# Sending the second head pair of four RWKV products to the other half of the array's columns

## The chip, the cores and the metric

The kernel runs on one core of one Trainium2 chip. Its time is the device time of that core in microseconds (us). Three runs of the kernel before took 2783.94, 2780.48 and 2779.83 us; the median is 2780.48 us. TensorE (called PE in the profile) multiplies matrices on an array of 128 x 128 cells and writes to PSUM, a memory of eight banks of 2 KB in each of 128 partitions. ScalarE (ACT) and VectorE (DVE) read PSUM and write SBUF, the main on-chip memory. A matmul may use a part of the array: the rows are given by the partitions from which its operands are read, the columns by the PSUM partitions to which its result goes.

## The reference, cut to what matters

One decoder layer over 2048 tokens of width 1024: a norm, one input projection, two groups of heads side by side (HGRN2, 4 heads of 128, and RWKV-7, 8 heads of 64), an output projection, and a feed-forward part with a short convolution. Everything is float32. The change touches RWKV-7 alone, whose recurrence is

```python
def step(S, inp):
    rt, wt, kt, vt, at, bt = inp
    sa = jnp.einsum('bhvk,bhk->bhv', S, at)
    S = S * wt[:, :, None, :] + sa[..., None] * bt[:, :, None, :] + vt[..., None] * kt[:, :, None, :]
    y = jnp.einsum('bhvk,bhk->bhv', S, rt)
    return S, y
```

## The kernel before

The kernel has two phases. Phase 1 (about the first 1400 us) makes the input projection, the two kinds of heads and the output projection; phase 2 is the feed-forward part, which the change doesn't touch.

Phase 1 is written as three Python generators. `dense` issues the projections: for each block of 512 tokens and each group of 128 output columns, 24 matmuls of 128x512 (L259 to L261: each float32 product is made of three products of rounded parts, which ACT and DVE split at L243 and L244 into `wh` and `wl`). `rw_stream` runs RWKV, `hg_stream` runs HGRN2. A loop takes one step (up to the next `yield`) of the RWKV generator, one of the HGRN2 generator, and then lets `dense` issue work worth `TICK` = 2000 ns. The framework's scheduler then orders the instructions of each engine once more, at build time, so instructions can move across the steps; at run time each engine works its list in order, and waits where an operand or a buffer isn't ready.

PSUM is split by tags: two banks for `dense` (`pj`), two for HGRN2 (`hg`), and two buffers of two banks each for RWKV (`rw`, taken by `bank2()`). A third `bank2()` waits until the reader of the first is done.

RWKV goes in eight steps called `rw_super`, two for each block of 512 tokens. One takes four heads, as two head pairs `u` = 0, 1 (a pair fills 128 partitions, head `h` = 0, 1 in it), and eight chunks of 64 tokens, numbered by `b` = 0 to 3 and `e` = 0, 1. Within a chunk the recurrence becomes a triangular system of 64 x 64, which is inverted. Matrices of chunk `e` live on the partitions 64 to 127 for `e` = 0 and 0 to 63 for `e` = 1 (`er0(e)` gives the first one). Each `rw_super` has four products that the change touches, each with one small matmul for every `(u, b, h, e)`, 32 in all:

- `lv` (L742): 64 rows by 64 columns of the array, 64 elements streamed. The rows begin at `kr`, the columns at `er0(e)`; one ACT instruction of 128x1024 copies the result to `RHS`.
- `z` (L786) and `z2` (L800): 32 rows by 32 columns, 32 streamed, which join the two inverted 32 x 32 halves of the triangular matrix. After each, two ACT instructions (one for each `e`) of 32x512 copy the result, to `TZ` and to `TTs`.
- `qu` (L814): 64 rows by 64 columns, 128 streamed. Head pair 0 is done first into one `bank2()`, and copied by three ACT instructions (one to `M`, two to `UV`), then a `yield`, and head pair 1 likewise, with a `yield` of its own.

In all four, both head pairs use the same two parts of the array: for `lv` and `qu` two of the four 64 x 64 quadrants, one for each `e`. The order within each product is all matmuls of head pair 0, then all of head pair 1.

After `qu` comes `yg` (L834): for each `u`, 32 matmuls of 64 rows by 64 columns with 64 streamed (16 with `M` as the streamed operand, 16 with `KBT`). In it the rows go by `e` and the columns by `h`, so that all four quadrants are used. `yg` of head pair 0 takes the `bank2()` that `qu` of head pair 0 held, and `yg` of pair 1 that of pair 1. Then come `xp` and `yp` (L850, L857), and the carry from chunk to chunk (L868, L870).

Between `lv` and `z` lies the inversion of the 32 x 32 blocks on DVE (31 pairs of instructions), and transfers through DRAM.

Of the kernel before, what the change touches and what calls it, by code (L numbers as in the profile page):

```python
# [11 lines left out]
AF = mybir.ActivationFunctionType  # L12
# [6 lines left out]
P = 128  # L19
# [42 lines left out]
def tile_layer(ctx, tc, consts, x, norm1_w, w_in, hg_lb_logits, hg_norm_w, rw_shift_mu, rw_w0, rw_w2,  # L62
# [4 lines left out]
    V, S, TE = nc.vector, nc.scalar, nc.tensor  # L67
# [41 lines left out]
    def act(out_, in_, func, **kw):  # L109

        want = tables.get(func)
        if want is not None and want != tab["now"]:
            pre = S.preload_act_table_set(want)
            for u_ in tab["uses"]:
                tc.add_manual_dep(pre.ins, u_.ins.name, NOSYNC, reason="table order")
            tab.update(now=want, pre=pre, uses=[])
        i_ = S.activation(out_, in_, func, **kw)
        if want is not None:
            tc.add_manual_dep(i_.ins, tab["pre"].ins.name, NOSYNC, reason="table order")
            tab["uses"].append(i_)  # L120
        return i_
# [141 lines left out]
    def phase1(c1):  # L263
# [14 lines left out]
        TTs = hp.tile([P, 16, 64], F32, name="TTs")  # L278
# [324 lines left out]


        er0 = lambda e: 64 if e == 0 else 0
        c16 = lambda t_: t_.rearrange("p u (c t) -> p (u c) t", t=64)
        v16 = lambda t_: t_.rearrange("p u (b e t) -> p (u b) e t", e=2, t=64)
        U = range(2)

        def rw_super(nb, s_):  # L610
# [6 lines left out]
            def tile_(tag, shape, name):  # L617
                return rp.tile([P] + shape, F32, tag=tag, name=name)

            def bank2():  # L620
                return ps.tile([P, 2, BLK], F32, tag="rw", name="rw", bufs=2)
# [3 lines left out]
            bs_ = [bank2() for _ in U]  # L625
            for u in U:
                TE.matmul(bs_[u][:, 0, :], w2a2[64:128, pc[u]], tl[64:128, :], start=True, stop=True)
            for u in U:
                TE.matmul(bs_[u][:, 1, :], w2a2[0:64, pc[u]], tl[0:64, :], start=True, stop=True)
            for u in U:  # L630
                act(a[:, u], bs_[u][:, 0, :], AF.Sigmoid, bias=vec("a0", prs[u]))
# [47 lines left out]
            M = tile_("M", [2, 2, 4, 2, P], "M")  # L679
            for j in range(2):  # L680
                for u in U:
                    s1 = bank2()
                    for i in range(4):
                        b, e = 2 * j + i // 2, i % 2
# [13 lines left out]
            for u in U:  # L698
                for e in range(2):
                    for q in range(2):  # L700
                        r0 = er0(e) + 32 * q
# [13 lines left out]
            RHS = tile_("KB", [8, 2, P], "RHS")  # L715
            UV = tile_("UV", [8, 2, P], "UV")
# [15 lines left out]
            yield  # L732

            lv = bank2()
            for u in U:
                for b in range(4):
                    for h in range(2):
                        for e in range(2):
                            kr = 0 if e == 0 else 64
                            r0 = er0(e)  # L740
                            sl = (b * 2 + h) * 64
                            TE.matmul(lv[r0:r0 + 64, u, sl:sl + 64], M[kr:kr + 64, u, e, b, h, 0:64],  # L742
                                      UV[kr:kr + 64, 4 * u + b, e, h * 64:h * 64 + 64], start=True, stop=True,
                                      tile_position=(kr, r0))
            act(RHS[:, :, :, 64:128], lv.rearrange("p u (b h t) -> p (u b) h t", h=2, t=64), AF.Copy)
            yield

            n = 64
# [17 lines left out]
            TZ = tile_("XH", [2, 2, 4, 2, 32], "TZ")  # L766
            for u in U:
                for e in range(2):
                    r0 = er0(e)
# [7 lines left out]
            for _ in range(2):  # L777
                yield
            z = bank2()
            for u in U:  # L780
                for b in range(4):
                    for h in range(2):
                        for e in range(2):
                            r0 = er0(e)
                            sl = u * 256 + (b * 2 + h) * 32
                            TE.matmul(z[r0 + 32:r0 + 64, 0, sl:sl + 32], M[r0:r0 + 32, u, e, b, h, 32:64],  # L786
                                      TZ[r0:r0 + 32, 0, u, b, h, :], start=True, stop=True,
                                      tile_position=(r0, r0 + 32))
            for e in range(2):
                r1 = er0(e) + 32  # L790
                act(TZ[r1:r1 + 32, 1].rearrange("p u b h t -> p (u b h t)"), z[r1:r1 + 32, 0, :], AF.Copy)
            yield
            z2 = bank2()
            for u in U:
                for b in range(4):
                    for h in range(2):
                        for e in range(2):
                            r0 = er0(e)
                            sl = u * 256 + (b * 2 + h) * 32
                            TE.matmul(z2[r0:r0 + 32, 0, sl:sl + 32], TZ[r0 + 32:r0 + 64, 1, u, b, h, :],  # L800
                                      TTs[r0 + 32:r0 + 64, u * 8 + b * 2 + h, 32:64], start=True, stop=True,
                                      tile_position=(r0 + 32, r0))
            for e in range(2):
                r0 = er0(e)
                act(TTs[r0:r0 + 32, :, 32:64], z2[r0:r0 + 32, 0, :].rearrange("p (s t) -> p s t", t=32), AF.Copy)
            yield
            for u in U:
                qu = bank2()
                for b in range(4):
                    for h in range(2):  # L810
                        for e in range(2):
                            r0 = er0(e)
                            sl = ((b % 2) * 2 + h) * P
                            TE.matmul(qu[r0:r0 + 64, b // 2, sl:sl + P], TTs[r0:r0 + 64, u * 8 + b * 2 + h, :],  # L814
                                      RHS[r0:r0 + 64, 4 * u + b, h, :], start=True, stop=True,
                                      tile_position=(r0, r0))
                quv = qu.rearrange("p j (b h t) -> p (j b) h t", h=2, t=P)
                bs = slice(4 * u, 4 * u + 4)
                act(M[:, u, 0, :, :, 0:64], quv[:, :, :, 0:64], AF.Copy)
                act(UV[64:128, bs, 0, :].rearrange("p b (h t) -> p b h t", t=64), quv[64:128, :, :, 64:128], AF.Copy)  # L820
                act(UV[0:64, bs, 1, :].rearrange("p b (h t) -> p b h t", t=64), quv[0:64, :, :, 64:128], AF.Copy)
                yield
            for u in U:
                Q, G = M[:, u, 0, :, :, 0:64], M[:, u, 1, :, :, 0:64]
                yg = bank2()
                for w in range(2):
                    for b in range(4):
                        for e in range(2):
                            rs_ = slice(er0(e), er0(e) + 64)
                            sl = w * 256 + b * 64  # L830
                            for h in range(2):
                                rhs = (M[rs_, u, e, b, h, 64:128] if w == 0
                                       else KBT[rs_, u, 2 * b + e, h * 64:h * 64 + 64])
                                TE.matmul(yg[h * 64:h * 64 + 64, e, sl:sl + 64], Q[rs_, b, h, :], rhs,  # L834
                                          start=True, stop=True, tile_position=(er0(e), h * 64))
# [10 lines left out]
            for u in U:  # L846
                for ch in range(8):
                    b, e = ch // 2, ch % 2
                    for h in range(2):
                        TE.matmul(xp[h * 64:h * 64 + 64, u, ch * 64:ch * 64 + 64], KBT[:, u, ch, h * 64:h * 64 + 64],  # L850
                                  UV[:, 4 * u + b, e, h * 64:h * 64 + 64], start=ch == 0, stop=False,
                                  tile_position=(0, h * 64), skip_group_check=True)
            for u in U:
                for ch in range(8):
                    b, e = ch // 2, ch % 2
                    for h in range(2):
                        TE.matmul(yp[h * 64:h * 64 + 64, u, ch * 64:ch * 64 + 64],  # L857
                                  UV[:, 4 * u + b, e, h * 64:h * 64 + 64], M[:, u, e, b, h, 64:128], start=ch == 0,
                                  stop=False, tile_position=(0, h * 64), skip_group_check=True)
            yield  # L860
            WC2 = WC.rearrange("p (u c) t -> p u c t", u=2)
            for ch in range(8):
                b, e = ch // 2, ch % 2
                cs_ = slice(ch * 64, ch * 64 + 64)
                for u in U:
                    for h in range(2):
                        hr = slice(h * 64, h * 64 + 64)
                        TE.matmul(xp[hr, u, cs_], M[hr, u, 1, b, e, 0:64], XH[hr, u, ch, :], start=False,  # L868
                                  stop=ch == 7, tile_position=(h * 64, h * 64), skip_group_check=True)
# [3 lines left out]
            for u in U:  # L873
                for ch in range(8):
                    cs_ = slice(ch * 64, ch * 64 + 64)
                    for h in range(2):
                        hr = slice(h * 64, h * 64 + 64)
                        TE.matmul(yp[hr, u, cs_], XH[hr, u, ch, :], RT[hr, u, ch, :], start=False, stop=ch == 7,
                                  tile_position=(h * 64, h * 64), skip_group_check=True)
# [186 lines left out]
    if "1" in stages:  # L1066
        with ExitStack() as c1:
            phase1(c1)
# [15 lines left out]
    with ExitStack() as c2:  # L1084
# [35 lines left out]
        with tc.tile_pool(name="op", bufs=1, reuse_waits="tile") as op_:  # L1120
# [4 lines left out]
            b = NBLK - 1  # L1125
# [248 lines left out]
    with tc.tile_pool(name="dn", bufs=1, reuse_waits="tile") as dn:  # L1374
# [59 lines left out]
        for s_ in range(3, N):  # L1434
            g, p, kk = steps[s_]
# [53 lines left out]
```

## Time and profile before

| | |
|---|---|
| time of three runs, median | 2780.48 us |
| profiled execution: span from the first to the last instruction (the page gives no other time for it) | 2783.2 us |
| PE busy over the span | 2678.8 us, 96% |
| ACT busy over the span | 1421.1 us, 51% |
| PE busy in phase 1 (0 to 1400 us) | 1335.72 us |
| mean granted TensorE clock | 0.984 of full speed |

A group of the profile is one line of the kernel on one engine with one shape; its row gives the count, the busy time, the mean duration of one in ns, and the idle time just ahead. A matmul that the code writes in float32 is two records in the trace, so 32 matmuls of `lv` are 64 records, and eight `rw_super` have 512. Ends of matmuls are modelled and overlap, so the pace of a burst is read from the start of its first to the start of what follows. A row of the timeline gives start, duration, engine, line, operation, shape and count, and in brackets how long the engine had been idle and for whom.

### The profile page before, as it was taken

How to read it: one execution, taken by the hardware profiler on the slowest of the kernel's cores; microseconds unless marked ns; L12 is line 12 of the kernel's file. 1: busy time of each engine (PE TensorE's matmuls, PEld its weight loads, DVE VectorE, ACT ScalarE, POOL GpSimd, SP SyncE). 2: the span in 40 equal slices, each digit the busy share in tenths (PEclk: the TensorE clock that was granted, in tenths of full speed). 3: DMA queues.
4: the chain of work that ended last, by engine and by line, in shares of the span. 5: the costliest groups of instructions: out<-in, count | busy, mean ns of one | idle time of the engine just before them, and what ended most of it. 6: DMA issues, size and time to landing. Idle time of an engine off the chain costs nothing.

```text
span 2783.2 us, 47784 instructions
## 1 busy us (share of the span) xinstructions
PE 2678.8 (96%) x18059; PEld 2135.2 (77%) x18059; DVE 2066.4 (74%) x3877; ACT 1421.1 (51%) x2254; POOL 11.1 (0%) x24
## 2 busy tenths in 40 slices
PE   8999999989999999999989999998999999999998
PEld 6877777767787777777767888886888888877887
DVE  4867778685686766868658789989997877677656
ACT  5445454544646446435346765456455555445444
POOL 0000000000000000000000000000000000000000
PEclk9999999999999999999899999999999999999999
DMA  5222322244441344543475457756672223998855
GB/s 163 72 69 72 99 73 78 63 131 141 131 121 58 102 141 136 161 132 94 131 239 178 143 172 262 239 165 216 205 245 88 87 76 135 324 333 310 289 193 186
DMA packets 429628, 435.01 MB, mean 156 GB/s; under 512 B 68703, under 2 KB 288213, under 8 KB 429397
## 3 DMA queue, kind: packets, MB, share of 16 engines
q1 hardware_dynamic: 428337, 429.30, 48.4%
q8 instruction: 142, 2.33, 0.3%
q0 software_dynamic: 992, 2.64, 0.2%
q14 instruction: 89, 0.73, 0.1%
q10 hardware_dynamic: 68, 0.02, 0.0%
HBM read 325.94 MB, written 105.91 MB: 155 GB/s over the span
## 4 chain that ended last, share of the span: by engine, by line
PE 78%; DVE 7%; ACT 7%; DMA 4%; issue 3%; SPq 1%; DVEq 0%; ACTq 0%
PE pj L259 8%; PE pj L260 8%; PE pj L261 8%; PE ua L261 6%; PE ua L259 5%; PE ua L260 5%; PE ud L259 3%; PE ud L260 3%; PE ud L261 3%; PE da L260 2%; PE da L261 2%; PE da L259 2%; PE hg L948 2%; PE db L259 2%; PE db L260 2%
## 5 line engine op out<-in xcount | busy, mean ns | idle before, releaser
L259 PE MATMUL pj<-hh,wh 128*128 128x512 f32 x960 | 401.8, 419 | 0.9 <-DVE xh L398 0.4
L260 PE MATMUL pj<-hl,wh 128*128 128x512 f32 x960 | 379.9, 396 | 0.0
L261 PE MATMUL pj<-hh,wl 128*128 128x512 f32 x960 | 379.0, 395 | 0.2 <-DVE wl L244 0.2
L243 ACT CAST wh<-wraw 128x512 fp32r<-128x512 f32 x240 | 147.0, 619 | 307.9 <-PE pj L260 266.2
L259 PE MATMUL ua<-Bh,uwh 128*128 128x512 f32 x704 | 278.6, 396 | 15.0 <-ACT uwh L243 13.7
L261 PE MATMUL ua<-Bh,uwl 128*128 128x512 f32 x704 | 276.6, 393 | 0.7 <-DVE uwl L244 0.7
L260 PE MATMUL ua<-Bl,uwh 128*128 128x512 f32 x704 | 276.5, 393 | 0.0
L244 DVE TENSOR_TENSOR wl<-wraw,wh 128x512 fp32r<-128x512 f32 x240 | 163.3, 686 | 133.8 <-ACT wh L243 132.9
L259 PEld LDWEIGHTS pj<-hh,wh 128*128 128x128 f32 x960 | 180.8, 188 | 53.1 <-issue 13.6
L260 PEld LDWEIGHTS pj<-hl,wh 128*128 128x128 f32 x960 | 180.9, 188 | 42.4 <-issue 7.9
L243 ACT CAST uwh<-uraw 128x512 fp32r<-128x512 f32 x220 | 134.9, 618 | 151.2 <-PE ua L260 80.0
L261 PEld LDWEIGHTS pj<-hh,wl 128*128 128x128 f32 x960 | 180.7, 188 | 39.9 <-issue 1.3
L243 ACT CAST dah<-draw 128x512 fp32r<-128x512 f32 x151 | 93.8, 621 | 182.7 <-PE da L260 50.5
L244 DVE TENSOR_TENSOR uwl<-uraw,uwh 128x512 fp32r<-128x512 f32 x220 | 146.9, 685 | 50.8 <-ACT uwh L243 50.8
L244 DVE TENSOR_TENSOR dal<-draw,dah 128x512 fp32r<-128x512 f32 x151 | 104.2, 690 | 107.0 <-ACT dah L243 106.8
L259 PEld LDWEIGHTS ua<-Bh,uwh 128*128 128x128 f32 x704 | 133.5, 190 | 44.0 <-ACT uwh L243 14.3
L261 PEld LDWEIGHTS ua<-Bh,uwl 128*128 128x128 f32 x704 | 133.6, 190 | 30.4 <-DVE uwl L244 2.3
L260 PEld LDWEIGHTS ua<-Bl,uwh 128*128 128x128 f32 x704 | 133.6, 190 | 27.2
L259 PE MATMUL ud<-Bh,uwh 128*128 128x512 f32 x352 | 137.9, 392 | 1.9 <-DVE cv L1340 1.9
L261 PE MATMUL ud<-Bh,uwl 128*128 128x512 f32 x352 | 137.1, 389 | 0.0
L260 PE MATMUL ud<-Bl,uwh 128*128 128x512 f32 x352 | 137.0, 389 | 0.0
L260 PE MATMUL da<-dbl,dah 128*128 128x512 f32 x340 | 133.5, 393 | 1.7 <-DVE dbl L244 1.6
(314 smaller groups left out, 5959.7 us busy)
## 6 DMA issues: line engine op xcount, KB each, us to landing
wraw<-in_w_in_dram SPq DMA_DIRECT2D x240, 256.0 KB, 3.0
uraw<-in_w_up_dram SPq DMA_DIRECT2D x176, 256.0 KB, 3.3
woraw<-in_w_out_dram SPq DMA_DIRECT2D x96, 256.0 KB, 3.1
draw<-Sg SPq DMA_DIRECT2D x88, 256.0 KB, 2.9
draw<-Tw SPq DMA_DIRECT2D x88, 256.0 KB, 3.0
gd<-y SPq DMA_DIRECT2D x86, 256.0 KB, 2.9
xt<-x1d SPq DMA_DIRECT2D x32, 512.0 KB, 6.6
draw<-gd SPq DMA_DIRECT2D x63, 256.0 KB, 5.1
```

Of the source, the lines that this page charges most:

```text
L243: S.copy(hi, src)
L244: V.tensor_sub(lo, src, hi.bitcast(F32))
L259: TE.matmul(acc, lh, rh, start=first, stop=False, skip_group_check=skip)
L260: TE.matmul(acc, lh, rl, start=False, stop=False, skip_group_check=skip)
L261: TE.matmul(acc, ll, rh, start=False, stop=last, skip_group_check=skip)
L948: TE.matmul(o, kt[:, t0:t0 + 64], qs, start=True, stop=True, tile_position=(0, e * 64))
```

## The change

In all four products the matmuls of head pair 1 get the columns that head pair 0 doesn't use with the same rows, and the order becomes `b, h, e, u`, so that four matmuls in a row go to four different parts of the array. The results of head pair 1 then lie in PSUM partitions in which they aren't wanted: chunk `e` in the half of the other `e` (for `z` and `z2` in a neighbouring 32). ACT instructions that read one partition range and write another put them back: `lv` is copied by three instructions (128x512 for pair 0, two of 64x512 for pair 1) where it was one, `z` and `z2` by four each of 32x256 where it was two of 32x512, and `qu` by seven where it was six, three for pair 0 and four for pair 1. `qu` takes both `bank2()` at its start, and one of its two `yield`s is gone. Apart from that, the first products of `rw_super` (L627, L629) are now written in one loop over `u` instead of two, which changes their order.

```diff
+        def quads():
+            return [(b, h, e, u) for b in range(4) for h in range(2) for e in range(2) for u in U]
+        def col0(u, e):
+            return er0(e) if u == 0 else 64 - er0(e)
...
             lv = bank2()
-            for u in U:
-                for b in range(4):
-                    for h in range(2):
-                        for e in range(2):
-                            kr = 0 if e == 0 else 64
-                            r0 = er0(e)
-                            sl = (b * 2 + h) * 64
-                            TE.matmul(lv[r0:r0 + 64, u, sl:sl + 64], M[kr:kr + 64, u, e, b, h, 0:64],
-                                      UV[kr:kr + 64, 4 * u + b, e, h * 64:h * 64 + 64], start=True, stop=True,
-                                      tile_position=(kr, r0))
-            act(RHS[:, :, :, 64:128], lv.rearrange("p u (b h t) -> p (u b) h t", h=2, t=64), AF.Copy)
+            for b, h, e, u in quads():
+                kr, c0, sl = 64 - er0(e), col0(u, e), (b * 2 + h) * 64
+                TE.matmul(lv[c0:c0 + 64, u, sl:sl + 64], M[kr:kr + 64, u, e, b, h, 0:64],
+                          UV[kr:kr + 64, 4 * u + b, e, h * 64:h * 64 + 64], start=True, stop=True,
+                          tile_position=(kr, c0))
+            lvv = lv.rearrange("p u (b h t) -> p u b h t", h=2, t=64)
+            act(RHS[:, 0:4, :, 64:128], lvv[:, 0], AF.Copy)
+            for e in range(2):
+                r0, c0 = er0(e), col0(1, e)
+                act(RHS[r0:r0 + 64, 4:8, :, 64:128], lvv[c0:c0 + 64, 1], AF.Copy)
...
             z = bank2()
+            for b, h, e, u in quads():
+                r0 = er0(e)
+                c0, sl = r0 + 32 - 32 * u, u * 256 + (b * 2 + h) * 32
+                TE.matmul(z[c0:c0 + 32, 0, sl:sl + 32], M[r0:r0 + 32, u, e, b, h, 32:64],
+                          TZ[r0:r0 + 32, 0, u, b, h, :], start=True, stop=True, tile_position=(r0, c0))
+            for u in U:
+                for e in range(2):
+                    r1 = er0(e) + 32
+                    c0 = r1 - 32 * u
+                    act(TZ[r1:r1 + 32, 1, u].rearrange("p b h t -> p (b h t)"),
+                        z[c0:c0 + 32, 0, u * 256:u * 256 + 256], AF.Copy)
...
-            for u in U:
-                qu = bank2()
...
-                act(M[:, u, 0, :, :, 0:64], quv[:, :, :, 0:64], AF.Copy)
-                act(UV[64:128, bs, 0, :].rearrange("p b (h t) -> p b h t", t=64), quv[64:128, :, :, 64:128], AF.Copy)
-                act(UV[0:64, bs, 1, :].rearrange("p b (h t) -> p b h t", t=64), quv[0:64, :, :, 64:128], AF.Copy)
-                yield
+            qus = [bank2() for _ in U]
+            for b, h, e, u in quads():
+                r0, c0, sl = er0(e), col0(u, e), ((b % 2) * 2 + h) * P
+                TE.matmul(qus[u][c0:c0 + 64, b // 2, sl:sl + P], TTs[r0:r0 + 64, u * 8 + b * 2 + h, :],
+                          RHS[r0:r0 + 64, 4 * u + b, h, :], start=True, stop=True, tile_position=(r0, c0))
+            for u in U:
+                quv = qus[u].rearrange("p j (b h t) -> p (j b) h t", h=2, t=P)
+                bs = slice(4 * u, 4 * u + 4)
+                if u == 0:
+                    act(M[:, u, 0, :, :, 0:64], quv[:, :, :, 0:64], AF.Copy)
+                for e in range(2):
+                    r0, c0 = er0(e), col0(u, e)
+                    if u == 1:
+                        act(M[r0:r0 + 64, u, 0, :, :, 0:64], quv[c0:c0 + 64, :, :, 0:64], AF.Copy)
+                    act(UV[r0:r0 + 64, bs, e, :].rearrange("p b (h t) -> p b h t", t=64),
+                        quv[c0:c0 + 64, :, :, 64:128], AF.Copy)
+            yield
```

More of the change, by code (lines that the diff above doesn't have):

```diff
@@ L779, in rw_super @@
             z = bank2()
-            for u in U:
[L781 to L788, printed above, removed]
@@ L789, in rw_super @@
-            for e in range(2):
-                r1 = er0(e) + 32
-                act(TZ[r1:r1 + 32, 1].rearrange("p u b h t -> p (u b h t)"), z[r1:r1 + 32, 0, :], AF.Copy)
+            for b, h, e, u in quads():
[3 more added lines that the diff above has]
+                          TZ[r0:r0 + 32, 0, u, b, h, :], start=True, stop=True, tile_position=(r0, c0))
@@ L792, in rw_super @@
+            for u in U:
+                for e in range(2):
[3 more added lines that the diff above has]
+                        z[c0:c0 + 32, 0, u * 256:u * 256 + 256], AF.Copy)
             yield
             z2 = bank2()
-            for u in U:
[L795 to L802, printed above, removed]
@@ L803, in rw_super @@
-            for e in range(2):
-                r0 = er0(e)
-                act(TTs[r0:r0 + 32, :, 32:64], z2[r0:r0 + 32, 0, :].rearrange("p (s t) -> p s t", t=32), AF.Copy)
-            yield
-            for u in U:
-                qu = bank2()
[L809 to L817, printed above, removed]
-                bs = slice(4 * u, 4 * u + 4)
-                act(M[:, u, 0, :, :, 0:64], quv[:, :, :, 0:64], AF.Copy)
-                act(UV[64:128, bs, 0, :].rearrange("p b (h t) -> p b h t", t=64), quv[64:128, :, :, 64:128], AF.Copy)
-                act(UV[0:64, bs, 1, :].rearrange("p b (h t) -> p b h t", t=64), quv[0:64, :, :, 64:128], AF.Copy)
-                yield
+            for b, h, e, u in quads():
+                r0 = er0(e)
+                c0, sl = r0 + 32 * u, u * 256 + (b * 2 + h) * 32
+                TE.matmul(z2[c0:c0 + 32, 0, sl:sl + 32], TZ[r0 + 32:r0 + 64, 1, u, b, h, :],
+                          TTs[r0 + 32:r0 + 64, u * 8 + b * 2 + h, 32:64], start=True, stop=True,
+                          tile_position=(r0 + 32, c0))
@@ new lines, in rw_super @@
+            for u in U:
+                for e in range(2):
+                    r0 = er0(e)
+                    c0 = r0 + 32 * u
+                    act(TTs[r0:r0 + 32, 8 * u:8 * u + 8, 32:64],
+                        z2[c0:c0 + 32, 0, u * 256:u * 256 + 256].rearrange("p (s t) -> p s t", t=32), AF.Copy)
+            yield
+            qus = [bank2() for _ in U]
+            for b, h, e, u in quads():
+                r0, c0, sl = er0(e), col0(u, e), ((b % 2) * 2 + h) * P
+                TE.matmul(qus[u][c0:c0 + 64, b // 2, sl:sl + P], TTs[r0:r0 + 64, u * 8 + b * 2 + h, :],
+                          RHS[r0:r0 + 64, 4 * u + b, h, :], start=True, stop=True, tile_position=(r0, c0))
@@ new lines, in rw_super @@
+            for u in U:
+                quv = qus[u].rearrange("p j (b h t) -> p (j b) h t", h=2, t=P)
+                bs = slice(4 * u, 4 * u + 4)
+                if u == 0:
+                    act(M[:, u, 0, :, :, 0:64], quv[:, :, :, 0:64], AF.Copy)
+                for e in range(2):
+                    r0, c0 = er0(e), col0(u, e)
[3 more added lines that the diff above has]
+                        quv[c0:c0 + 64, :, :, 64:128], AF.Copy)
```

## The prediction, made before the changed kernel had run

> **What bounds the kernel now.** I read the page's busy times first, then the chain that ended last, then the busy time by stage, and then the groups and the timeline of the lines that the diff touches.
>
> ```profile
> span 2783.2 us, 47784 instructions
> PE 2678.8 (96%) x18059; PEld 2135.2 (77%) x18059; DVE 2066.4 (74%) x3877; ACT 1421.1 (51%) x2254; POOL 11.1 (0%) x24
> PE 78%; DVE 7%; ACT 7%; DMA 4%; issue 3%; SPq 1%; DVEq 0%; ACTq 0%
> ```
>
> ```profile
> 0.00:1400.00 1400.00, 1335.72 (x12143) 1038.26 (x12144) 998.73 (x2269) 694.48 (x1098) 8.74 (x20) 0.98 0.37 109
> ```
>
> The second fence is the row of phase 1: stretch, its length, then busy time (and count) of PE, PEld, DVE, ACT and POOL, the granted clock, DMA share and GB/s. PE is busy for 1335.72 of 1400 us at a granted clock of 0.98, and the chain lies on PE for 78%. ACT has half of phase 1 free. So in phase 1 a microsecond of PE that goes away is worth nearly one of the span, as long as PE finds something else to do at that place; a microsecond more on ACT costs only where PE waits for that very instruction.
>
> The groups of the four products and of `yg`, with the loop lines of the kernel before:
>
> ```profile
> L742 PE MATMUL rw<-UV,M 64*64 64x64 f32 x512 | 17.9, 220 | 0.6 <-ACT UV L117 0.3
> L786 PE MATMUL rw<-TZ,M 32*32 32x32 f32 x512 | 16.2, 204 | 0.0
> L800 PE MATMUL rw<-TTs,TZ 32*32 32x32 f32 x512 | 13.9, 209 | 1.7 <-ACT TZ L117 1.7
> L814 PE MATMUL rw<-RHS,TTs 64*64 64x128 f32 x512 | 38.0, 295 | 0.0
> L834 PE MATMUL rw<-M 64*64 64x64 f32 x512 | 11.5, 224 | 5.4 <-ACT UV L117 4.5
> L834 PE MATMUL rw<-KBT,M 64*64 64x64 f32 x512 | 10.8, 219 | 0.0
> ```
>
> The four touched products hold PE for 17.9 + 16.2 + 13.9 + 38.0 = 86 us: all that could be won here is a share of 3% of the span. The row to look at is L834: the same shape as L742, the same count, but 11.5 and 10.8 us in place of 17.9, and it is the one that already uses four quadrants.
>
> **Part 1: `lv` in four quadrants.** The pace, from the timeline of PE (start, duration, line, count):
>
> ```profile
> 259.71 2.50 PE L742 MATMUL rw<-UV,M 64*64 64x64 f32 x64
> 262.14 0.50 PE L259 MATMUL pj<-hh,wh 128*128 128x512 f32 x1
> ...
> 414.84 2.08 PE L742 MATMUL rw<-UV,M 64*64 64x64 f32 x64
> 416.86 0.50 PE L259 MATMUL pj<-hh,wh 128*128 128x512 f32 x1
> ```
>
> ```profile
> 320.97 1.00 PE L948 MATMUL hg<-hX 128*64 128x32 f32 x26
> ...
> 324.51 0.69 PE L786 MATMUL rw<-TZ,M 32*32 32x32 f32 x30
> 325.13 0.50 PE L260 MATMUL pj<-hl,wh 128*128 128x512 f32 x1
> ...
> 327.09 1.19 PE L800 MATMUL rw<-TTs,TZ 32*32 32x32 f32 x62
> 328.22 0.50 PE L260 MATMUL pj<-hl,wh 128*128 128x512 f32 x1
> ...
> 328.79 0.39 PE L259 MATMUL pj<-hh,wh 128*128 128x512 f32 x1
> 329.02 0.40 PE L260 MATMUL pj<-hl,wh 128*128 128x512 f32 x1
> ...
> 330.37 3.70 PE L814 MATMUL rw<-RHS,TTs 64*64 64x128 f32 x62
> 334.22 0.69 PE L834 MATMUL rw<-M 64*64 64x64 f32 x32
> 334.73 0.65 PE L834 MATMUL rw<-KBT,M 64*64 64x64 f32 x32
> 335.98 0.69 PE L834 MATMUL rw<-M 64*64 64x64 f32 x32 [0.60 <-ACT UV L117]
> 336.49 0.65 PE L834 MATMUL rw<-KBT,M 64*64 64x64 f32 x32
> 337.07 2.08 PE L850 MATMUL rw<-UV,KBT 128*64 128x64 f32 x64
> ```
>
> A burst of `lv` takes 2.02 to 2.43 us for 64 records, 32 to 38 ns each. `yg` takes 334.73 - 334.22 = 0.51 us for 32, 16 ns each, with the same 64x64 tiles in the same order of quadrants (two columns of one row half, then of the other). Counted per quadrant the two agree (2 x 32 = 64 ns against 4 x 16 = 64 ns), so I read the bound as one quadrant's own pace. At 16 ns `lv` takes 64 x 16 = 1.03 us. Per `rw_super` the gain is 1.0 to 1.4 us. The group rows give a smaller one, 17.9 - 11.2 = 6.7 us in all eight; the burst rows up to 8 x 1.2 = 9.6. I take 8.
>
> **Part 2: `z` and `z2`.** These go at (325.13 - 324.51) / 30 = 21 ns and (328.22 - 327.09) / 62 = 18 ns with two parts of the array. That is near the 16 ns which is the shortest pace of any small matmul that I found in this trace, so I can't tell whether four parts would go faster. Bounds: nothing, or half of both groups' bursts, (0.62 + 0.62 + 1.13) / 2, some 1.2 us in each `rw_super`. I take nothing, since the nearest row (16 ns) is a floor as far as this trace shows. The Trainium skill has a rule that speaks against gains at this size: its page "TensorE: Matmul & The Clock Gate", in "Wait — 56ns, not 53.3ns?", says that start-to-start never falls below about 25 ns however short the matmul. By it `lv` would end at 64 x 25 = 1.6 us and win only some 0.5 us each time (4 us in all, and the whole sum would be 4 us smaller); the L834 rows, 32 starts in 0.51 us, don't agree with it, so the row decides.
>
> **Part 3: `qu`.** 62 records in 334.22 - 330.37 = 3.85 us, 60 ns each with two quadrants; the nearest row for four quadrants is `yg`, which halves. So 62 x 30 = 1.9 us, and PE would be rid of 1.95 us in each `rw_super`. But here what comes after is late next, since `yg` needs the copies that ACT makes:
>
> ```profile
> 332.36 0.60 ACT L117 ACTIVATE M<-rw 128x512 f32<-128x512 f32 x1 [2.19 <-PE rw L814]
> 332.97 1.20 ACT L117 ACTIVATE UV<-rw 64x512 f32<-64x512 f32 x2
> 334.11 0.60 ACT L117 ACTIVATE M<-rw 128x512 f32<-128x512 f32 x1
> 334.73 1.20 ACT L117 ACTIVATE UV<-rw 64x512 f32<-64x512 f32 x2
> ```
>
> ```profile
> PE rw L834 <- ACT UV L117: 4.5, 7, 1.1
> PE pj L259 <- ACT wh L243: 7.7, 10, 1.7
> ```
>
> Before, ACT copies pair 0 while PE computes pair 1, and only 0.60 us of waiting is left ahead of `yg` of pair 1 (335.98; 4.5 us in all eight). After, both pairs end together, and seven copies of 0.60 follow: 4.2 us. `yg` of pair 0 takes over the banks of `qu` of pair 0, so it waits for three copies, 1.8 + 0.2 us for the hand-overs; `yg` of pair 1 waits for all seven, 4.4 us after the end of `qu`. `yg` of pair 0 itself fills 1.1 us of that. The rest is filled only by what the scheduler put between `qu` and `yg`. The instruction order of the changed program has there, in the eight `rw_super`: 5 dense matmuls and 11 of HGRN2; 3 and 24; 9 and 0; 8 and 1; 4 and 24; 8 and 0; 3 and 8; 4 and 1. At 0.23 us for a dense one (329.02 - 328.79) and 2 x 0.038 for one of HGRN2 (26 records in 1.00) that is 2.0, 2.5, 2.1, 1.9, 2.7, 1.8, 1.3 and 1.0 us, 1.9 in the mean. So from the start of `qu` to the end of `yg` of pair 1: 1.9 + 4.4 + 1.1 = 7.4 us, of which 1.9 us is other work done, leaves 5.5. Before, it is 337.07 - 330.37 = 6.7 us with nothing else in it. The gain is 1.2 us, not 1.95: 9.6 us in all eight. Ends: 0.8 us worse each time if the matmuls keep their pace (last rival), 1.95 better if the waits cost nothing.
>
> What is queued behind the waiting `yg` on PE is everything: dense and HGRN2 matmuls too, as the list is worked in order. What is queued behind the seven copies on ACT is mostly a cast `wh` for the next dense weights. Weights for some matmuls are cast ahead; when that cover is gone, the price is the second wait row, 7.7 us over 10 times, longest 1.7.
>
> **Part 4: the copies of `z` and `z2`, of `lv`, and the smaller edits.**
>
> ```profile
> L117 ACT ACTIVATE TZ<-rw 32x512 f32<-32x512 f32 x16 | 9.4, 590 | 19.0 <-PE rw L786 18.8
> L117 ACT ACTIVATE Af<-hg 64x256 f32<-64x256 f32 x16 | 6.0, 374 | 2.0 <-PE hg L992 1.9
> L117 ACT ACTIVATE RHS<-rw 128x1024 f32<-128x1024 f32 x8 | 8.2, 1027 | 8.4 <-PE rw L742 8.4
> ```
>
> Two copies of 590 ns become four of about 374 (the row of the same 256 elements from PSUM): 1.18 becomes 1.50 us, 0.32 us more between `z` and `z2`, and the same between `z2` and `qu`. In the changed order some dense or HGRN2 work stands in each of these gaps, but before, too, it doesn't always suffice (1.7 us of waits in the L800 row). I charge half of it: 16 x 0.16 = 2.5 us; ends 0 and 5. The copies of `lv` grow from 1.03 to 3 x 0.60 = 1.8 us. Nobody needs `RHS` before `qu`, and between lie 31 pairs of DVE instructions, so I charge nothing; without that cover it would be 0.8 us each, 6 us. In all ACT gets 0.77 + 0.32 + 0.32 + 0.60 = 2.0 us more each, 16 us in all, beside 1400 - 694 = 706 us free in phase 1. The order of L627 and L629 changes only in the four of eight places where it didn't already alternate: nothing. No DMA and no DVE work is added or removed.
>
> The `yield` that is gone takes 2000 ns of dense budget from this place in each of the eight steps. The work isn't lost; it moves later. Whether it is missed or fills an idle stretch there I can't see from the trace of before. All of PE's idle time in phase 1 is 1400 - 1336 = 64 us, 8 us for each `rw_super`; I take no change and put 1 us either way on each step, 8 us, into the range.
>
> **Sum.** -8 (`lv`) + 0 (`z`, `z2`) - 9.6 (`qu` with its waits) + 2.5 (copies) = -15 us. Against the profiled execution, whose span is 2783.2 us and whose time outside the span isn't given, that is 2768; its span lies 2.7 us over the median of the three runs, 2780.5, and from that I get 2765 us.
>
> **Rivals.** *All of the pace is kept*: other work covers the waits ahead of `yg`, and `z` and `z2` gain too. For it: a scheduler chose the fillers. Against: they sum to 1.9 us where 3.3 is needed. -9.6 - 8 x 1.95 - 4 = -29: 2751 us.
>
> *The waits and the moved work eat it*: in each of the eight, `yg`, `z2` and `qu` wait some 1.5 us longer than I charged, because less is ready behind the lost `yield`. -15 + 12 = -3, within 0.2% (5.6 us, about what a measurement of this kernel can tell from no change): 2777 us. For it: the 12.4 us between the two bounds of `qu` and `z`. Against: copies stand back to back in the changed order of ACT.
>
> *Slower: the four parts don't overlap.* Place: L742 and L814. In `yg` each row half has its own bank; in the changed `lv` and `qu` both row halves write into each bank at once, into different partitions. If such writes exclude each other, `lv` stays at 32 ns or more and `qu` at 60. Then `qu` ends after 3.85 us, and only then the seven copies start: 3.85 + 4.4 + 1.1 - 1.9 = 7.45 against 6.7, 0.75 us worse each, with the copies of `z` 6 + 2.5 = +8.5: 2789 us. It decides as soon as `qu` stays above about 52 ns per record (a burst of 3.3 us) and `lv` wins nothing. Against it: `lv` before has both row halves in one bank too, and per quadrant it is as fast as `yg` (64 ns). The Trainium skill states that rule in "TensorEngine Tiling (Array Packing)", section "Restrictions and Gotchas": different row tiles can't access one PSUM bank at the same time. No row of this trace shows such an exclusion, so the rival gets a small chance.
>
> **How the numbers follow.** My forecast 0.60, all of the pace 0.13, eaten 0.15, not overlapping 0.12. The likeliest is 2765, its own range 2757 to 2773 (the 8 us of moved work). For 8 in 10 the range takes in the first rival and the second and leaves most of the last out: 2751 to 2781. Faster by over 0.2%: 0.60 and 0.13, 0.73; within: most of the second rival, 0.13; slower: the rest of it and the last rival, 0.14.
>
> **What would show it.** `lv` with 64 records in 1.0 to 1.2 us, `qu` with 62 in about 1.9, its group at some 20 us in place of 38; `z` and `z2` bursts unchanged; `yg` waits for ACT at 1 us or more in most `rw_super`, about 10 us in all in place of 4.5; ACT busy 16 us longer; PE busy in phase 1 some 25 us less at these lines. The prediction is wrong if `qu` stays at 60 ns, or if dense matmuls (`pj`) wait for `wh` or for evictions much longer than 7.7 us.

## The result, and the profile after

The changed kernel takes 2764.26 us in the median of four runs (2761.54 to 2768.94), the kernel before 2780.15 beside it (2779.82 to 2783.94): a ratio of 0.9937, with a 95% interval of 0.9916 to 0.9958. A second series (below) gave 0.9932 (0.9915 to 0.9949). The forecast was 2765. The sum behind it holds less well than its total, as the parts show.

The page of the changed kernel, its first lines; and the groups on PE of the four products and of `yg`. Their lines are now L745 (`lv`), L790 (`z`), L803 (`z2`), L816 (`qu`) and L841 (`yg`).

```profile
span 2765.2 us, 47846 instructions
PE 2650.8 (96%) x18059; PEld 2107.8 (76%) x18059; DVE 2067.1 (75%) x3877; ACT 1426.2 (52%) x2304; POOL 11.1 (0%) x24
```

```profile
L745 PE MATMUL rw<-UV,M 64*64 64x64 f32 x512 | 11.0, 222 | 0.5
L790 PE MATMUL rw<-TZ,M 32*32 32x32 f32 x512 | 10.3, 207 | 1.7 <-DMA TZ<-Td 1.7
L803 PE MATMUL rw<-TTs,TZ 32*32 32x32 f32 x512 | 9.7, 205 | 0.6 <-ACT TZ L117 0.4
L816 PE MATMUL rw<-RHS,TTs 64*64 64x128 f32 x512 | 23.7, 311 | 0.0
L841 PE MATMUL rw<-M 64*64 64x64 f32 x512 | 11.5, 229 | 9.8 <-ACT UV L117 9.8
```

The four groups fall from 17.9, 16.2, 13.9 and 38.0 us to 11.0, 10.3, 9.7 and 23.7: 31.3 us of PE less. PE is busy for 2678.8 - 2650.8 = 28.0 us less. But the span is only 18.0 us shorter, so PE idles 10 us more (span less busy: 104.4 before, 114.4 after). Half of that stands in the last row: `yg` waits 9.8 us for the copies, where it was 4.5. Other rows of the waits of phase 1 on PE (who waited for whom, us in all, times, longest) hold most of the rest, some up and some down:

```profile
PE rw L841 <- ACT UV L117: 9.8, 10, 2.1
PE hg L997 <- DVE hk L990: 9.3, 6, 2.9
PE rw L695 <- DVE KB L683: 4.4, 6, 1.1
PE hg L955 <- DVE hk L916: 4.1, 2, 2.9
PE hg L955 <- DVE hX L934: 3.2, 5, 1.2
PE pj L427 <- ACT xt L117: 1.9, 8, 0.4
```

The same rows of the kernel before:

```profile
PE hg L990 <- DVE hk L983: 6.8, 3, 2.9
PE pj L427 <- ACT xt L117: 4.9, 6, 1.3
PE rw L687 <- DVE KB L675: 0.8, 2, 0.5
PE hg L948 <- DVE hk L909: 0.5, 1, 0.5
PE hg L948 <- DVE hX L927: 0.5, 2, 0.3
```

PE waits 2.5 and 3.6 us longer at two places for HGRN2's `hk`, 2.7 longer for its `hX` and 3.6 longer for RWKV's `KB`, all made by DVE, and 3.0 less for `xt`, which ACT makes. DVE's own work (2067 us) stayed, so a faster PE can come to it sooner. That isn't the whole reason: the waits for `KB` and at the second place for `hk` are 4.0 and 3.0 us in the pair-by-pair kernel with two `yield`s below, too, where the four products still take 80.1 of their 86.0 us. So the new order of the instructions has a share in them.

The second `rw_super` of the changed kernel on PE, to be read against the rows from 320.97 us on in the prediction:

```profile
309.67 0.70 PE L790 MATMUL rw<-TZ,M 32*32 32x32 f32 x58
310.30 0.50 PE L261 MATMUL pj<-hh,wl 128*128 128x512 f32 x1
...
314.95 2.02 PE L816 MATMUL rw<-RHS,TTs 64*64 64x128 f32 x62
316.90 1.59 PE L955 MATMUL hg<-hX 128*64 128x32 f32 x48
318.42 0.50 PE L259 MATMUL pj<-hh,wh 128*128 128x512 f32 x1
...
319.31 0.69 PE L841 MATMUL rw<-M 64*64 64x64 f32 x32
319.83 0.65 PE L841 MATMUL rw<-KBT,M 64*64 64x64 f32 x32
321.06 0.69 PE L841 MATMUL rw<-M 64*64 64x64 f32 x32 [0.58 <-ACT UV L117]
...
322.44 2.09 PE L857 MATMUL rw<-UV,KBT 128*64 128x64 f32 x64 [0.22 <-DVE AR L847]
```

`qu` takes 1.95 us for 62 records, 31 ns each (60 before). `z` takes 0.63 us for 58, 11 ns each (21 before). Then 2.4 us of HGRN2 and dense matmuls fill the wait for the first three copies, and PE still idles 0.58 us ahead of `yg` of pair 1. `yg` ends at 322.44 - 0.22 = 322.22. From the start of `qu` that is 7.3 us with 2.4 us of other work in it, 4.9 net against 6.7. ACT at the same place (the seven copies, back to back):

```profile
317.02 0.60 ACT L117 ACTIVATE M<-rw 128x512 f32<-128x512 f32 x1 [2.06 <-PE rw L816]
317.63 1.20 ACT L117 ACTIVATE UV<-rw 64x512 f32<-64x512 f32 x2
318.85 0.59 ACT L117 ACTIVATE M<-rw 64x512 f32<-64x512 f32 x1
319.34 0.58 ACT L117 ACTIVATE UV<-rw 64x512 f32<-64x512 f32 x1
319.93 0.59 ACT L117 ACTIVATE M<-rw 64x512 f32<-64x512 f32 x1
320.43 0.58 ACT L117 ACTIVATE UV<-rw 64x512 f32<-64x512 f32 x1
```

They start 0.12 us after `qu` and end at 321.01, where `yg` of pair 1 begins at 321.06.

### The profile page after: what moved, and what is told of

The parts are those of the page before. It is cut to its first block, busy times and chain, and to the rows that moved or that the text cites. A ratio compares the mean times of both kernels' runs of the same rounds, so it can differ in the third digit from the quotient of the medians.

```text
span 2765.2 us, 47846 instructions
## 1 busy us (share of the span) xinstructions
PE 2650.8 (96%) x18059; PEld 2107.8 (76%) x18059; DVE 2067.1 (75%) x3877; ACT 1426.2 (52%) x2304; POOL 11.1 (0%) x24
```

## The experiments

The two theories at the start: *the terms* (each part is worth the PE time that it frees, less the waits that the prediction charged), against *the order* (how the scheduler's list shifts decides, and the parts don't add up). All ratios are against the kernel before, run on the same chip between the others; the interval is 95%.

**One product at a time.** The edits are the parts of the diff for `lv`, for `z` with `z2`, and for `qu`, each put alone into the kernel before.

> Of the four products only lv has the change (its columns, its order, its three copies). As predicted (each part is worth its own PE time): lv falls from 17.9 to some 11 us of PE, nothing waits for it, so the time falls by 6 to 8 us, to about 2773. Rival (the parts are not worth their PE time, what decides is how the scheduler's order shifts): anything between 2770 and 2785 with the same 11 us in lv's group.

> Only z and z2 have the change (columns, order, four copies each). The prediction gave these nothing on PE and 2.5 us of cost in copies: about 2783. The trace of the changed kernel shows their groups at 10.3 and 9.7 us in place of 16.2 and 13.9; by that theory 10 us less PE against 2.5 us for the copies: about 2773. By the rival that order shifts decide, it can be either.

> Only qu has the change (columns, order, both buffers at once, seven copies, one yield less). As predicted: qu's group falls from 38 to about 21 us, the waits of yg for copies grow from 4.5 to about 10 us, net -9.6: about 2771. Rival A (waits and the lost yield eat it): 2777 to 2783. Rival B (all of its pace is kept): 2765. If e1, e2 and e3 add up to the -16 of the whole, the parts are independent.

| alone | ratio (interval) | in us | PE time of its groups, before to alone |
|---|---|---|---|
| `lv` | 0.9990 (0.9979 to 1.0002) | -2.8 | 17.9 to 10.6 |
| `z`, `z2` | 0.9995 (0.9984 to 1.0006) | -1.4 | 30.1 to 20.7 |
| `qu`, with the lost `yield` | 0.9966 (0.9955 to 0.9978) | -9.5 | 38.0 to 23.8 |

Every group falls as in the whole. The times sum to -13.7 us, the whole gave -17.5, and each carries some 3 us of uncertainty, so the parts may well add up. But neither `lv` nor `z` brings the microseconds that it frees. Of `z` alone, the groups and a wait:

```profile
L791 PE MATMUL rw<-TZ,M 32*32 32x32 f32 x512 | 10.4, 205 | 0.8 <-DMA TZ<-Td 0.8
L804 PE MATMUL rw<-TTs,TZ 32*32 32x32 f32 x512 | 10.3, 211 | 3.3 <-ACT TZ L117 3.2
```

```profile
PE rw L857 <- DVE AR L847: 5.9, 4, 1.9
```

PE waits 3.2 us for the copies of `z` where it was 1.7, and `xp` (L857) 5.9 us for DVE where it was 2.7. I read this as PE coming to the next hand-over sooner and waiting there; the longer copies of `z` are in the first of the two waits as well. None of the three kernels has the reordered L627 and L629, and no run has that edit alone.

**The order of the matmuls.** In the changed kernel, head pair 0 is again done ahead of pair 1; columns, copies and the single `yield` stay.

```diff
         def quads():
-            return [(b, h, e, u) for b in range(4) for h in range(2) for e in range(2) for u in U]
+            return [(b, h, e, u) for u in U for b in range(4) for h in range(2) for e in range(2)]
```

> The changed kernel, with the 32 matmuls of each of the four products in the old order: all of head pair 0, then all of pair 1. Tiles, copies and the single yield are those of the changed kernel. If the gain needs neighbouring matmuls to go to different quadrants, lv goes back to 32 to 38 ns per record, qu to 60, z and z2 to 18 to 21, and what is left is the price of the copies and of the lost yield: 2781 to 2792, about 2786 as the sum +2.5 for copies and +0.4 each for qu's copies would have it. If columns alone did it, about 2765.

Measured: 0.9988 (0.9979 to 0.9997), 2777.6 us. Groups of the pair-by-pair kernel, and a burst of `qu` with the row after it:

```profile
L816 PE MATMUL rw<-RHS,TTs 64*64 64x128 f32 x512 | 32.2, 289 | 0.0
L745 PE MATMUL rw<-UV,M 64*64 64x64 f32 x512 | 16.9, 222 | 0.5
L790 PE MATMUL rw<-TZ,M 32*32 32x32 f32 x512 | 15.9, 204 | 0.3 <-DMA TZ<-Td 0.3
L803 PE MATMUL rw<-TTs,TZ 32*32 32x32 f32 x512 | 12.2, 204 | 0.1
```

```profile
164.96 3.33 PE L816 MATMUL rw<-RHS,TTs 64*64 64x128 f32 x62
168.22 0.65 PE L955 MATMUL hg<-hX 128*64 128x32 f32 x14
```

`lv` and `z` go back nearly to their old times. `qu` goes to 3.26 us, 53 ns per record: not quite the old 60, for a reason that I don't know. So most of the gain on PE needs neighbouring matmuls in different quadrants; with the other columns alone the four groups take 77.2 us, against 86.0 before and 54.7 with the turn through the quadrants. But the time didn't go over that of before, as I had expected. With all copies and longer waits of `yg` (8.9 us) this kernel is 3 us faster than before. The groups that are still 9 us shorter can be a part of that. So can the clock: its mean over all runs was 0.98583 against 0.98455 for the kernel before beside it, and 0.00128 x 2780 is 3.6 us, an estimate as large as the whole gain. The one other thing in the change that could be worth several us, and that can be tested alone, is the `yield`.

**The `yield`, and the waits of `yg`.** Four kernels on one chip: the changed one again; with the second `yield` put back behind the one after `qu`; with the two copies to `UV` of pair 1 on DVE; and with a `yield` after each `yg` instead of one after both.

```diff
                     act(UV[r0:r0 + 64, bs, e, :].rearrange("p b (h t) -> p b h t", t=64),
                         quv[c0:c0 + 64, :, :, 64:128], AF.Copy)
             yield
+            yield
...
-                    act(UV[r0:r0 + 64, bs, e, :].rearrange("p b (h t) -> p b h t", t=64),
-                        quv[c0:c0 + 64, :, :, 64:128], AF.Copy)
+                    uv_o = UV[r0:r0 + 64, bs, e, :].rearrange("p b (h t) -> p b h t", t=64)
+                    uv_i = quv[c0:c0 + 64, :, :, 64:128]
+                    if u == 1:
+                        V.tensor_copy(uv_o, uv_i)
+                    else:
+                        act(uv_o, uv_i, AF.Copy)
...
                 V.tensor_add(RTe, ygv[:, 0], RTe)
-            yield
+                yield
```

> The changed kernel as it is, beside the three variants of it. As measured before: 2764, a ratio of 0.993 to 0.994. If its parts (lv, z, qu alone: -2.9, -1.4 and -9.5 us) simply add up, 0.995 (2767); a ratio under that by more than the interval would mean that the parts help each other.

> The changed kernel with the second yield put back behind the copies of qu, so that each of the eight steps gets its 2000 ns of dense budget again. The prediction gave the lost yield no price (within 8 us). By that the time stays within 3 us of the changed kernel. Rival: the lost yield is what made the pair-by-pair kernel 3 us faster than before although it has all the copies; then putting it back costs 3 to 8 us (2768 to 2772).

> The changed kernel with the two copies to UV of head pair 1 made by VectorE in place of ScalarE, so that five copies of 0.6 us, not seven, stand between the end of qu and yg of pair 1. If the copies set the waits of yg, as predicted (4.4 us after qu becomes 3.2), the 9.8 us that yg waits for copies fall to 3 to 5 us and the time falls by 3 to 7 us, to 2757 to 2761. Rival (PE idles elsewhere instead, since VectorE's own chain in phase 1 gets 11 us longer): no change or slower, 2763 to 2768.

> The changed kernel with one yield between yg of pair 0 and yg of pair 1 in addition to the one behind them, so that the loop's dense budget stands in the gap in which PE waits for the last copies. If that gap is worth filling and the scheduler keeps the work there, the waits of yg fall from 9.8 by some 5 us and the time by as much (2759). If the scheduler moves it, waits and time stay as they are.

| kernel | ratio (interval) | median us |
|---|---|---|
| changed, again | 0.9932 (0.9915 to 0.9949) | 2765.2 |
| with the second `yield` | 0.9960 (0.9946 to 0.9974) | 2773.4 |
| two copies on DVE | 0.9926 (0.9907 to 0.9946) | 2763.9 |
| `yield` in `yg` | 0.9954 (0.9937 to 0.9971) | 2774.2 |

A `yield` more costs 8 or 9 us by the medians and 8 or 6 by the ratios, in whichever of the two places it stands; the intervals of the ratios just overlap. I had priced it at nothing. In the gap between the two `yg` it didn't fill the wait: `yg` waits 8.0 us for its copies there, and 8.0 with the second `yield` behind `qu`. The copies on DVE didn't bring what I expected: `yg` now waits for DVE instead.

```profile
PE rw L845 <- DVE UV L830: 8.2, 7, 2.7
PE rw L845 <- ACT UV L117: 3.0, 2, 2.1
```

That is 11.2 us of waiting in place of 9.8, and a time that can't be told from that of the changed kernel. None of the variants tried here clearly beats it.

**Is the `yield` worth as much without the quadrants?** The kernel before with a single `yield` behind `qu` of both pairs; the pair-by-pair kernel with two; and, to see whether it is the amount of dense work per step that counts, the kernel before and the one with copies on DVE with `TICK` lowered, so that some 35 steps of 60 ns take away as much as one `yield`.

```diff
                 act(UV[0:64, bs, 1, :].rearrange("p b (h t) -> p b h t", t=64), quv[0:64, :, :, 64:128], AF.Copy)
-                yield
+            yield
...
-TICK = 2000.0
+TICK = 1940.0
```

> The kernel before with one edit: the yield behind qu stands once behind both head pairs, as in the changed kernel, with the old columns, order, buffers and six copies. Putting the second yield back into the changed kernel cost 8 us. If that is a price of its own, this kernel is 8 us faster than before (ratio 0.997). Rival: the yield matters only where qu is short and yg waits for seven copies; then no change (0.999 to 1.001).

> The changed kernel with the matmuls in the old order (pair 0, then pair 1) and with the second yield put back: what is left of the change is the columns, the copies and both buffers at once. Pair by pair with one yield had a ratio of 0.9988. If the yield is worth 8 us everywhere, 1.0015 to 1.002 (+5 us: the price of copies and waits that the prediction put at 2.5 plus qu's waits). If the yield is worth nothing here, 0.9988.

> The kernel before with TICK at 1940 in place of 2000 ns: about the same dense budget is taken from each of the eight steps (some 35 ticks x 60 ns = 2.1 us) as with one yield less, but spread over all of them. If what the yield changes is how much dense work is spent before PE would otherwise be idle, this is 4 to 8 us faster than before. If it is the one place behind qu, or the luck of one order, no change or either sign.

> The changed kernel with the two copies to UV of pair 1 on VectorE and TICK at 1940. If less dense budget per tick helps, it is the fastest of all, 2756 to 2760; if not, as with VectorE's copies alone, 2764, or slower.

| kernel | ratio (interval) | median us |
|---|---|---|
| before, one `yield` | 0.9980 (0.9970 to 0.9990) | 2781.1 |
| pair by pair, two `yield`s | 0.9999 (0.9987 to 1.0011) | 2784.4 |
| before, `TICK` 1940 | 1.0041 (1.0028 to 1.0054) | 2796.5 |
| copies on DVE, `TICK` 1940 | 0.9969 (0.9959 to 0.9979) | 2777.1 |

(The kernel before took 2784.9 on this chip.) With these the change comes apart:

| | two `yield`s | one `yield` |
|---|---|---|
| old columns and copies, pair by pair | 1 (before) | 0.9980 |
| new columns and copies, pair by pair | 0.9999 | 0.9988 |
| new columns and copies, quadrants in turn | 0.9960 | 0.9932 (changed) |

Down the columns from the second row to the third, the turn through the quadrants is worth 0.0039 and 0.0056, some 11 to 16 us, and these intervals are clear of each other. From the first row to the second, new columns with their copies, both buffers at once and the reordered L627 and L629 change nothing that can be measured (0.9999, and 0.0008 on the right). That is a net: the four groups are 6 us shorter there with two `yield`s (80.1 against 86.0), so the copies may cost something that this pays for. Across the rows, the lost `yield` is worth 0.0020, 0.0011 and 0.0028: 3 to 8 us, the middle one within its uncertainty of some 0.0015. A lower `TICK` makes both kernels slower, by 0.0041 and 0.0043, 11 and 12 us; that speaks against less dense work per step as the reason, though it shifts the order of the instructions as well.

Why the `yield` helps is only half answered. For the changed kernel with one and with two `yield`s, PE's busy time and the granted clock (the pages' lines, then the rows of span and mean clock):

```profile
PE 2648.3 (96%) x18059; PEld 2103.6 (76%) x18059; DVE 2067.3 (75%) x3877; ACT 1426.6 (52%) x2304; POOL 11.1 (0%) x24
...
core 0: 2763.7 us, clock 0.985
```

```profile
PE 2656.3 (96%) x18059; PEld 2108.3 (76%) x18059; DVE 2066.0 (75%) x3877; ACT 1434.7 (52%) x2310; POOL 11.1 (0%) x24
...
core 0: 2771.6 us, clock 0.982
```

PE idles equally long in both (2763.7 - 2648.3 = 115.4 us, 2771.6 - 2656.3 = 115.3). The whole difference is in busy time, with the same matmuls, and the clock says why: (1 - 0.985) x 2763.7 = 41 us are lost to a lower clock in one, (1 - 0.982) x 2771.6 = 50 us in the other. In the kernel before with one `yield`, it was the idle time that fell (from 104.4 to 99.0 us), at a mean clock of 0.983 against 0.984. Over all runs of the first pair the mean clocks are 0.9845 and 0.9828: 0.0017 x 2770 = 4.7 of the 8 us, and not all of them. With the clock's part taken off all six kernels of the table in this way (an estimate: the mean time less (1 - clock) x span, against the same for the kernel before beside it), the turn through the quadrants is worth 15 us with two `yield`s and 17 with one, and the lost `yield` 2 to 5.

One thing does change with the `yield` in every pair. `act` loads another table of functions on ACT (L113) whenever the next function in program order belongs to another set than the last. One `yield` less shifts RWKV's steps against HGRN2's, and with them the order of the functions. The kernel before, then the changed one:

```profile
L113 ACT ACT_TABLE_LOAD x61 | 78.3, 1283 | 1.8 <-PEq L1474 0.7
L113 ACT ACT_TABLE_LOAD x55 | 70.6, 1283 | 1.7 <-PEq L1481 0.7
```

A load takes 1283 ns. At `TICK` 2000, each kernel with one `yield` behind `qu` makes 55 of them, and each with two, or with one more in `yg`, makes 61. With 61, PE waits 4.2 to 4.9 us for `xt` (L427), up to 1.3 at a time; with 55 it waits 1.7 to 1.9 us, at most 0.4. For `hf`, which is copied just before, it waits 1 us more, so 1.3 to 2 us are left. In the kernel before, one of the longest of these waits stands behind a load (ACT, then PE):

```profile
229.88 1.28 ACT L113 ACT_TABLE_LOAD   x1
231.83 0.66 PE L427 MATMUL pj<-ident,xt 128*128 128x128 f32 x4 [1.25 <-ACT xt L117]
```

The two kernels with the lower `TICK` make 63 and 67 loads. So in each of these comparisons more loads go with the longer time, but not in proportion (two more in a kernel that is 11.5 us slower), and no run changes the loads alone. They are a candidate for a part of it; why the `yield` helps stays open.

## Why the prediction was right or wrong

**The bound.** "A microsecond of PE that goes away is worth nearly one of the span" was the step that failed most, and with it the condition behind it, that PE finds something else to do at that place. The four products freed 31 us of PE. From pair by pair to quadrants in turn, the groups fall from 77.2 to 54.2 us with one `yield` (32.2 + 16.9 + 15.9 + 12.2, against 23.3 + 11.0 + 10.2 + 9.7 in the second series), and 0.0056 of 2786 us, 16 us, comes off the time; with two `yield`s it is 25 us of PE for 11 us. So a microsecond was worth 0.4 to 0.7 of one. The prediction named the one wait that takes its place ahead of `yg`, and its size was right (about 10 us in all, 9.8 measured); the waits for DVE (`hk`, `hX`, `KB`) it didn't see.

**`lv`.** Right in size on PE: -8 taken, -6.9 measured. Five of eight bursts take 1.5 us and not 1.0 to 1.2, though at full clock, for a reason that no run shows; two take 1.1 and one 1.24. One of the five:

```profile
250.21 1.57 PE L745 MATMUL rw<-UV,M 64*64 64x64 f32 x64
251.71 0.50 PE L259 MATMUL pj<-hh,wh 128*128 128x512 f32 x1
```

Alone it brought 3 us of time, not 8.

**`z` and `z2`.** Wrong: "I take nothing, since the nearest row (16 ns) is a floor as far as this trace shows". They go at 11 ns per record, and freed 10 us. The prediction had the right reading at hand and didn't use it here: a quadrant's own pace. `z` before took 2 x 21 = 42 ns per record in one part of the array; with four parts that gives 10.5. What looked like a floor was the pace of a 64 x 64 part. In time, though, `z` alone brought only 1.4 us (-0.0005, and the interval reaches over zero), so the wrong term hardly hurt the sum.

**`qu` with its waits.** -9.6 taken, -9.5 measured alone. That looks exact and isn't: the measured one holds the lost `yield`, which by itself is worth 5.6 us in the kernel before. What is left for `qu`, some 4 us with an uncertainty as large, is less than the step said. Its own terms were right (31 ns per record against 30, seven copies of 0.59, a net 4.9 us against 5.5 in the second `rw_super`; the old 3.85 us for 62 records are 62 ns each, where the prediction has 60). But two of the eight bursts of `qu` fell where the clock was at half and took 4.05 and 4.10 us, so its group came to 23.7 us and not to some 20.

**The copies.** 2.5 us charged, and no cost measured that stands out (0.9999 for all the copies with two `yield`s, net of 6 us less in the groups). In the changed kernel `z2` waited less than before for `TZ` (0.4 against 1.7 us), with `z` alone more (3.2). On ACT the copies grew by 15.9 us, as forecast, but ACT as a whole is only 5.1 us busier (1426.2 against 1421.1): the six table loads that are gone took 7.7 us off, and other groups the rest.

**The lost `yield`.** "I take no change": wrong, 3 to 8 us of gain, for a reason that stays open. It was inside the 8 us that the range kept for it.

**The rivals.** That the parts don't overlap in one bank is refuted: `lv` and `qu` have both row halves in each bank and take some 0.6 of their time, and `z` has all four parts in one bank. The rule that the Trainium skill states in "TensorEngine Tiling (Array Packing)", "Restrictions and Gotchas" (different row tiles can't access one bank at once), isn't seen here as a loss of time when their partitions differ. Nor is the 25 ns that the Trainium skill gives in "TensorE: Matmul & The Clock Gate", "Wait — 56ns, not 53.3ns?", as the least time from start to start: 58 records, which are 29 written matmuls, start within 0.63 us, 22 ns for each written one. The L834 rows that the prediction set against this rule speak against it only if each record counts: 16 written matmuls in 0.51 us are 32 ns each. The other two rivals, 2751 us with all of the pace kept and 2777 with most of it eaten, lie outside the four runs (2761.5 to 2768.9); the waits did eat about half of what PE gained.

So the total, -15 taken and -16 to -19 measured, is partly luck; it came out of three errors that cancel: PE time counted at nearly its full worth (too much), 10 us of `z` left out and the `yield` left out (too little).

## What to carry to other kernels

For small float32 matmuls, find the pace of one part of the array (the burst's time per record times the parts in use) and divide by the parts that can run in turn; neighbours in the instruction order must go to different parts, as other columns alone brought little here. Then don't book the freed PE time as time: in this kernel with its several chains 0.4 to 0.7 of it came back, so look for the waits behind. An edit to a generator's steps changes the order of everything after it, here worth 3 to 8 us of a gain of 16 to 19, and no reading of the trace of before told its sign: test it by itself. Where an engine loads tables of functions, count the loads before and after.

## What the runs showed of the hardware

In places the granted clock falls to half after a stretch in which PE often waits, and a product that falls there loses what it gained. In the changed kernel, `qu` of the fourth `rw_super` takes 4.05 us for 64 records where the second takes 1.95 for 62:

```profile
598.96 1.07 PE L955 MATMUL hg<-hX 128*64 128x32 f32 x16 [1.48 <-DVE hX L935]
...
611.51 4.13 PE L816 MATMUL rw<-RHS,TTs 64*64 64x128 f32 x64
615.56 0.50 PE L260 MATMUL pj<-wl,hh 128*128 128x512 f32 x1
```

The rows by stretch there (length, busy PE, PEld, DVE, ACT, POOL, then the clock):

```profile
596.00:600.00 4.00, 1.95 (x34) 1.65 (x34) 3.97 (x14) 0.00 (x0) 0.00 (x0) 0.80 0.41 64
600.00:605.00 5.00, 3.17 (x95) 2.81 (x94) 4.52 (x15) 0.49 (x2) 0.00 (x0) 0.50 0.39 116
610.00:615.00 5.00, 5.00 (x64) 4.16 (x64) 1.29 (x2) 1.64 (x5) 0.00 (x0) 0.50 0.48 157
```

PE is busy for about half of 596 to 600 us, and the clock is at 0.50 from 600 us on, though PE then is busy for most of the time. Not every such stretch does it: in the kernel before, PE is busy for 2.79, 3.61 and 3.29 us of the three times 5 us from 600 to 615, and the clock stays at 1.00. It has stretches at half the clock too (630 to 635 us at 0.50), so a part of every difference here is where they fall. The kernel with `TICK` at 1940 has the lowest mean clock of all, 0.9805 in its six runs against 0.9839 for the kernel before: 0.0034 x 2796 = 9.5 of its 11.5 us.
